# Moving ScalarE's unused elementwise results, the id sums and the row totals from SBUF to PSUM in a segment-mean kernel

## Chip, cores and metric

The kernel runs on one core of one Trainium2 chip. The metric is the device time of one execution in microseconds (us), lower is better. SBUF and PSUM are the two on-chip memories in which tiles are placed (`cpool` and `ppool` below); VectorE, ScalarE and GpSimd are engines, each with its own list of instructions. Most executions of a kernel lie within about 2% here, so kernels were compared on one chip in alternating rounds. A few single runs lay more than 1.5% above the fastest of their kernel; these count as slow, and ranges in brackets show them. Ratios are taken from the fast runs that were not profiled.

## The reference

```python
n, num_segments = 10_000_000, 10000
data = np.random.randn(n).astype(np.float32)
segment_ids = np.sort(np.random.randint(0, num_segments, n))     # int64, sorted

sums, counts = np.zeros(num_segments), np.zeros(num_segments)    # float32
np.add.at(sums, segment_ids, data)
np.add.at(counts, segment_ids, 1)
return sums / np.maximum(counts, 1)
```

The ids are sorted, so each segment is one contiguous stretch of about 1000 values.

## The kernel before

Each of the 128 partitions holds 78,125 consecutive values and works on them as 90 rows of 875 (the last has 250). A row holds at most one border between two segments in the ordinary case, so per row two numbers are enough: the total of the row, and the sum of the part before the border. To find the border, the kernel does not read all ids. It reads five probes per row, a *first look* at them on VectorE gives a position, GpSimd gathers 175 ids there, ScalarE sums these ids, and from the sum a *second look* on VectorE gives the exact border. Then a *split* on VectorE sums the data before the border, while ScalarE makes the row's total.

```python
# cut; the constants are put in one line
P, L, W, NR, HALVES = 128, 875, 175, 90, 66
...
GS = cpool.tile([P, NR], FP32, name="GS")          # id sums, one column a row (SBUF)
T = cpool.tile([P, NR], FP32, name="T")            # row totals               (SBUF)
iota = ppool.tile([P, 1024], FP32, name="iota")    # PSUM already
...
junk_v = cpool.tile([P, L], BF16, name="junk_v")
junk_a = cpool.tile([P, L], BF16, name="junk_a")   # elementwise results that nobody reads (SBUF)

def add_ids(r):                                    # ScalarE, line 315
    nc.scalar.activation(
        out=junk_a[:, 0:W], in_=gt32[:, r % RING, 0 : 2 * W : 2], func=ACT.Copy,
        accum_out=GS[:, r : r + 1],
    )

def second_look(a, b):                             # VectorE, line 322
    def s1():
        nc.vector.scalar_tensor_tensor(
            out=KK[:, a:b], in0=YY[:, a:b], scalar=float(S // K), in1=GS[:, a:b],
            op0=ALU.mult, op1=ALU.subtract,
        )
        ...

def total(r):                                      # ScalarE, line 335
    ...
    d = tiles[r // 2][:, (r % 2) * L : (r % 2) * L + n]
    t = T[:, r : r + 1]
    nc.scalar.activation(out=junk_a[:, 0:n], in_=d, func=ACT.Copy, accum_out=t)

def split(r):                                      # VectorE, line 340
    ...                                            # n and d as in total
    nc.vector.scalar_tensor_tensor(
        out=junk_v[:, 0:n], in0=iota[:, 0:n], scalar=KK[:, r : r + 1], in1=d,
        op0=ALU.is_lt, op1=ALU.mult, accum_out=A[:, r : r + 1],
    )
```

The totals are read by VectorE in few places: once early (line 410), four times in `sums` (`B = T - A`, line 584) and twice at the very end in `inject` (line 751).

```python
# order of the loop (cut): rows of ids run 6 rows ahead of the data (5 rows from row 66 on)
for r in range(..., NR):
    ...                                            # loads of probes and data run further ahead
    while r >= -1 and gs < NR and gs <= r + x_sum(gs):
        add_ids(gs); gs += 1
    if r >= 0:
        total(r)
        split(r)
        for f in after[r]:                         # a second look every 6 rows, every 3 from row 66 on;
            f()                                    # first looks, later stages, the output
```

A second look for rows `a..b-1` stands after the split of row `a-1`. Waits between engines are put in by the framework, from which instruction touches which tile. For PSUM the unit is a bank (here, a tile of 2 KiB per partition): a reader of one column also waits for writes to the others. For an SBUF tile the waits go by columns (e8). Each `activation` with `accum_out` runs as two instructions, an ACTIVATE and an accumulator read (ACTIVATION_READ_ACCUMULATOR) that delivers the sum.

Of the kernel before, what the change touches and what calls it, by code (L numbers as in the profile page):

```python
# [9 lines left out]
FP32 = mybir.dt.float32  # L10
BF16 = mybir.dt.bfloat16
# [6 lines left out]
P = 128  # L18
D = 78125
L = 875  # L20
S = 175
K = L // S
NR = 90
# [95 lines left out]
def kernel(  # L119
# [16 lines left out]
    cpool = ctx.enter_context(tc.tile_pool(name="cpool", bufs=1))  # L136
# [3 lines left out]
    ppool = ctx.enter_context(tc.tile_pool(name="ppool", bufs=1, space=bass.MemoryType.PSUM))  # L140
# [100 lines left out]
    ST = cpool.tile([P, NR], FP32, name="ST")  # L241
    YY = cpool.tile([P, NR], FP32, name="YY")
    IDX = cpool.tile([P, NR], I32, name="IDX")
    GS = cpool.tile([P, NR], FP32, name="GS")
    T = cpool.tile([P, NR], FP32, name="T")
    tl = cpool.tile([P, 1], FP32, name="tl")
    NBP = cpool.tile([P, NX + 1], FP32, name="NBP")
    NB = NBP[:, 1:]
# [3 lines left out]
    nc.vector.memset(NBP, 0.0)  # L252
    nc.vector.memset(FFP[:, 0:1], 0.0)
    junk_v = cpool.tile([P, L], BF16, name="junk_v")
    junk_a = cpool.tile([P, L], BF16, name="junk_a")

    def first_look(g):

# [55 lines left out]
    def add_ids(r):  # L314
# [5 lines that stand above are left out]
    def second_look(a, b):  # L320
# [4 lines that stand above are left out]
# [6 lines left out]
    def total(r):  # L331
        n = min(L, D - r * L)
# [3 lines that stand above are left out]
# [71 lines left out]
    def extend():  # L407

        def s1():
            nc.vector.tensor_sub(out=B[:, 0:E], in0=T[:, 0:E], in1=A[:, 0:E])  # L410
            nc.vector.tensor_copy(out=V[:, 0 : E + 1], in_=VI[:, 0 : E + 1])
            edges(0, E)
# [168 lines left out]
    def sums(a, b, weigh=True, upto=NR):  # L581
        def s1():
            c = min(b, upto)
            nc.vector.tensor_sub(out=B[:, a:c], in0=T[:, a:c], in1=A[:, a:c])  # L584

# [163 lines left out]
    def inject(r, wt, wa, o):  # L749
        return [  # L750
            lambda: v.scalar_tensor_tensor(  # L751
                out=most, in0=wt, scalar=T[:, r : r + 1], in1=most, op0=ALU.mult, op1=ALU.add
            ),
# [158 lines left out]
```

## Time and profile before

| | before |
|---|---|
| median of 3 runs (lowest to highest) | 189.5 us (188.91 to 191.78) |
| profiled run / its span | 188.19 us / 186.4 us |
| VectorE busy / ScalarE busy | 140.8 us / 136.6 us |
| data rate in most slices up to 172 us | 300 to 345 GB/s |
| a ScalarE row (two ACTIVATEs and two reads) | 1.54 us |
| the last second look starts | 173.49 us |

The costliest groups, the waits and part of the tail stand in the prediction. Two more views belong to the reading. The first is the strip of the page: 40 slices of the span, each digit the busy share of a slice in tenths; then, from the list of DMA issues, the gathers with their median time from issue to landing.

```profile
DVE  6321397979197796858879997686899989999881
ACT  8010599967999497895959949599886786989940
...
GT<-in_segment_ids_dram,IDX POOLq DMA_INDIRECT x90, 6.4
```

From slice 7 to slice 27 both engines have slices that are full beside slices that are not, as engines have that wait for each other in a ring (first look, gather, id sums, second look). From slice 29 on VectorE is nearly full. The second view is the timeline around one second look of that tail, the one ahead of row 75; columns are start, length, engine, line, operation, and in brackets the idle time just before with what ended it.

```profile
156.99 0.33 DVE L322 SCALAR_TENSOR_TENSOR q<-YY,GS 128x3 f32<-128x3 f32 x1
...
157.31 0.94 ACT L335 ACTIVATE junk_a<-data_t 128x875 bf16<-128x875 f32 x1
157.36 1.13 DVE L340 SCALAR_TENSOR_TENSOR junk_v<-iota,q,data_t 128x875 bf16<-128x875 f32 x1
...
158.15 0.19 ACT L335 ACTIVATION_READ_ACCUMULATOR junk_a<-data_t 128x1 f32 x1
```

VectorE begins the second look at 156.99 without an idle time. ScalarE's total of row 74, which stands before it in the program, begins only at 157.31 and is complete at 158.34. Nothing ties the two: VectorE is 1.35 us ahead.

### The profile page before, as it was taken

Reading aid. Unit: us, or ns where it says so; the run is one execution under the profiler, and the core shown is the slowest. Engines: PE = TensorE matmul, PEld = TensorE weight load, DVE = VectorE, ACT = ScalarE, POOL = GpSimd, SP = SyncE. Lnnn points to the kernel's source line nnn. Section 1 sums busy time; section 2 is a strip of 40 time slices with the busy share of each in tenths; the row PEclk is TensorE's granted clock in tenths of the full one; section 3 lists DMA queues with packets and bytes.
Section 4 is the critical chain, followed back from the end, with each engine's and each line's share of the span. In section 5 each row is a group of like instructions: output and inputs, shape, how many; then the busy total and the mean of one; then the engine's idle time right before and its main releaser. Section 6 shows DMA issues by size and latency. Waiting matters only on the chain.

```text
span 186.4 us, 1479 instructions
## 1 busy us (share of the span) xinstructions
PE 1.6 (1%) x6; PEld 1.4 (1%) x6; DVE 140.8 (76%) x438; ACT 136.6 (73%) x362; POOL 99.9 (54%) x119
## 2 busy tenths in 40 slices
PE   0000000000002000000000000000000000010000
PEld 0000000000001000000000000000000000010000
DVE  6321397979197796858879997686899989999881
ACT  8010599967999497895959949599886786989940
POOL 5687775076734828266471664727347287883000
DMA  6999999999999999999999999999998999999000
GB/s 28 178 178 340 331 325 328 306 341 330 316 330 319 338 333 305 326 335 332 314 310 335 318 328 317 329 344 307 326 246 246 343 405 406 405 406 391 15 0 12
DMA packets 70613, 54.63 MB, mean 293 GB/s; under 512 B 60464, under 2 KB 61032, under 8 KB 70599
## 3 DMA queue, kind: packets, MB, share of 16 engines
q1 hardware_dynamic: 64667, 40.50, 73.8%
q0 software_dynamic: 5760, 14.01, 23.5%
q14 instruction: 14, 0.11, 0.2%
q10 hardware_dynamic: 172, 0.00, 0.1%
HBM read 56.59 MB, written 0.04 MB: 304 GB/s over the span
## 4 chain that ended last, share of the span: by engine, by line
DMA 33%; issue 32%; ACT 14%; POOL 13%; DVE 4%; POOLq 1%; ACTq 0%
DMA GT<-in_segment_ids_dram,IDX 23%; POOL GT L305 12%; DMA data_t<-in_data_dram 10%; ACT junk_a L335 9%; ACT junk_a L315 5%; POOLq L305 1%; DVE jj L236 0%; POOL i_i L198 0%; DVE junk_v L340 0%; DVE most L745 0%; DVE add L737 0%; POOL pb L703 0%; DVE sel L648 0%; DVE most L751 0%; POOL KL L689 0%
## 5 line engine op out<-in xcount | busy, mean ns | idle before, releaser
L305 POOL DMA_INDIRECT GT<-in_segment_ids_dram,IDX x90 | 90.9, 1010 | 66.9 <-ACT junk_a L315 33.5
L340 DVE SCALAR_TENSOR_TENSOR junk_v<-iota,q,data_t 128x875 bf16<-128x875 f32 x90 | 100.6, 1118 | 8.0 <-DMA data_t<-in_data_dram 6.7
L335 ACT ACTIVATE junk_a<-data_t 128x875 bf16<-128x875 f32 x90 | 83.6, 929 | 3.7 <-DMA data_t<-in_data_dram 0.7
L315 ACT ACTIVATE junk_a<-GT 128x175 bf16<-128x175 int32 x90 | 32.4, 360 | 38.1 <-DMA GT<-in_segment_ids_dram,IDX 35.9
L322 DVE SCALAR_TENSOR_TENSOR q<-YY,GS 128x6 f32<-128x6 f32 (+1 forms) x19 | 3.3, 171 | 21.7 <-ACT junk_a L315 21.7
L315 ACT ACTIVATION_READ_ACCUMULATOR junk_a<-GT 128x1 f32 x90 | 16.8, 187 | 0.0
L335 ACT ACTIVATION_READ_ACCUMULATOR junk_a<-data_t 128x1 f32 x90 | 16.8, 186 | 0.0
L340 DVE DVE_READ_ACCUMULATOR junk_v<-iota,q,data_t 128x1 f32 x90 | 7.4, 83 | 0.0
L272 DVE TENSOR_REDUCE SG<-pr 128x6 f32<-128x30 int32 x15 | 2.7, 180 | 5.7 <-DMA snt<-in_segment_ids_dram 3.3
L281 DVE TENSOR_SCALAR far<-ST 128x6 f32<-128x6 f32 x15 | 2.7, 178 | 0.5
L187 ACT ACTIVATE GT<-q 128x3150 int32<-128x3150 f32 x1 | 3.0, 2996 | 0.0
L284 DVE TENSOR_TENSOR ST<-ST,far 128x6 f32<-128x6 f32 x15 | 2.6, 170 | 0.5
L288 DVE SCALAR_TENSOR_TENSOR IDX<-ST,wb 128x6 int32<-128x6 f32 (+2 forms) x16 | 2.6, 165 | 0.5
L275 DVE SCALAR_TENSOR_TENSOR ST<-pr,SG 128x6 f32<-128x6 int32 x15 | 2.5, 166 | 0.5
L291 DVE SCALAR_TENSOR_TENSOR YY<-ST,SG 128x6 f32<-128x6 f32 x15 | 2.4, 161 | 0.0
L187 ACT ACT_TABLE_LOAD x1 | 1.3, 1283 | 0.7 <-PEq L896 0.7
L584 DVE TENSOR_TENSOR q<-T,q 128x44 f32<-128x44 f32 (+3 forms) x4 | 0.7, 178 | 1.4 <-ACT junk_a L335 1.4
L704 POOL TENSOR_SCALAR pb<-pb 128x168 f32<-128x168 f32 (+1 forms) x2 | 1.6, 784 | 0.2
L544 PE MATMUL badp<-bads,ones 128*128 128x1 f32 x2 | 0.6, 362 | 104.7 <-DVE bads L543 104.7
L236 DVE CAST jj<-jj_i 128x128 f32<-128x128 int32 x1 | 0.8, 840 | 0.7 <-POOL jj_i L235 0.7
L571 DVE RECIPROCAL ct<-ct 128x16 f32<-128x16 f32 (+2 forms) x4 | 1.2, 300 | 0.1
L544 PEld LDWEIGHTS badp<-bads,ones 128*128 128x128 f32 x2 | 0.5, 310 | 104.8 <-DVE bads L543 104.8
(129 smaller groups left out, 45.2 us busy)
## 6 DMA issues: line engine op xcount, KB each, us to landing
data_t<-in_data_dram SPq DMA_DIRECT2D x44, 875.0 KB, 10.6
GT<-in_segment_ids_dram,IDX POOLq DMA_INDIRECT x90, 6.4
pr<-in_segment_ids_dram SPq DMA_DIRECT2D x41, 10.0 KB, 8.1
data_t<-in_data_dram SPq DMA_DIRECT2D x1, 437.5 KB, 18.6
data_t<-in_data_dram SPq DMA_DIRECT2D x1, 125.0 KB, 15.8
out_dram<-OUT SPq DMA_DIRECT2D x1, 36.6 KB
pr<-in_segment_ids_dram SPq DMA_DIRECT2D x1, 31.0 KB, 4.0
snt<-in_segment_ids_dram ACTq DMA_DIRECT2D x1, 1.0 KB
```

The source lines that it names most:

```text
L187: nc.scalar.activation(out=gt32[:, :, 0 : 2 * W : 2], in_=view(q5[:, 0, 0:1], [[0, RING], [0, W]]), func=ACT.Copy)
L272: v.tensor_reduce(out=SG[:, a:b], in_=pr32[:, a:b, 0 : 2 * K : 2], axis=AX.X, op=ALU.add)
L275: v.scalar_tensor_tensor(out=ST[:, a:b], in0=VI[:, a + 1 : b + 1], scalar=float(K), in1=SG[:, a:b], op0=ALU.mult, op1=ALU.subtract,)
L281: v.tensor_scalar(out=far, in0=ST[:, a:b], scalar1=0.0, scalar2=FAR, op0=ALU.is_equal, op1=ALU.mult)
L284: v.tensor_add(out=ST[:, a:b], in0=ST[:, a:b], in1=far)
L288: v.scalar_tensor_tensor(out=IDX[:, c:d], in0=ST[:, c:d], scalar=float(w), in1=wb[:, c:d], op0=ALU.mult, op1=ALU.add)
L291: v.scalar_tensor_tensor(out=YY[:, a:b], in0=ST[:, a:b], scalar=float(K + 1), in1=SG[:, a:b], op0=ALU.mult, op1=ALU.add)
L305: nc.gpsimd.indirect_dma_start(out=GT[:, r % RING, :], out_offset=None, in_=ids2d[:], in_offset=bass.IndirectOffsetOnAxis(ap=IDX[:, r : r ...
L315: nc.scalar.activation(out=junk_a[:, 0:W], in_=gt32[:, r % RING, 0 : 2 * W : 2], func=ACT.Copy, accum_out=GS[:, r : r + 1],)
L322: nc.vector.scalar_tensor_tensor(out=KK[:, a:b], in0=YY[:, a:b], scalar=float(S // K), in1=GS[:, a:b], op0=ALU.mult, op1=ALU.subtract,)
L335: nc.scalar.activation(out=junk_a[:, 0:n], in_=d, func=ACT.Copy, accum_out=t)
L340: nc.vector.scalar_tensor_tensor(out=junk_v[:, 0:n], in0=iota[:, 0:n], scalar=KK[:, r : r + 1], in1=d, op0=ALU.is_lt, op1=ALU.mult, accum_ ...
```

## The change

The intent is to shorten ScalarE's writes: its unused elementwise results, and the sums that it delivers, are written to PSUM in place of SBUF. `junk_a` becomes a tile of 4 KiB per partition; the id sums and the totals share one tile of 2 KiB, that is, one bank in the sense above. The order of instructions on every engine stays as it was.

```diff
-    GS = cpool.tile([P, NR], FP32, name="GS")
-    T = cpool.tile([P, NR], FP32, name="T")
+    GST = ppool.tile([P, 2, 256], FP32, name="GST")
+    GS, T = GST[:, 0, 0:NR], GST[:, 1, 0:NR]
...
-    junk_a = cpool.tile([P, L], BF16, name="junk_a")
+    junk_a = ppool.tile([P, 1024], FP32, name="junk_a")
```

## The prediction

> **What bounds the kernel now.** I read the page first: busy shares, the DMA row, the costliest groups.
>
> ```profile
> PE 1.6 (1%) x6; PEld 1.4 (1%) x6; DVE 140.8 (76%) x438; ACT 136.6 (73%) x362; POOL 99.9 (54%) x119
> ...
> DMA  6999999999999999999999999999998999999000
> ...
> L340 DVE SCALAR_TENSOR_TENSOR junk_v<-iota,q,data_t 128x875 bf16<-128x875 f32 x90 | 100.6, 1118 | 8.0 <-DMA data_t<-in_data_dram 6.7
> L335 ACT ACTIVATE junk_a<-data_t 128x875 bf16<-128x875 f32 x90 | 83.6, 929 | 3.7 <-DMA data_t<-in_data_dram 0.7
> L315 ACT ACTIVATE junk_a<-GT 128x175 bf16<-128x175 int32 x90 | 32.4, 360 | 38.1 <-DMA GT<-in_segment_ids_dram,IDX 35.9
> L322 DVE SCALAR_TENSOR_TENSOR q<-YY,GS 128x6 f32<-128x6 f32 (+1 forms) x19 | 3.3, 171 | 21.7 <-ACT junk_a L315 21.7
> L315 ACT ACTIVATION_READ_ACCUMULATOR junk_a<-GT 128x1 f32 x90 | 16.8, 187 | 0.0
> L335 ACT ACTIVATION_READ_ACCUMULATOR junk_a<-data_t 128x1 f32 x90 | 16.8, 186 | 0.0
> ```
>
> No compute engine is full. The DMA engines are busy in nearly every slice up to 172 us, but busy queues alone do not say what ends a step. VectorE (DVE) idles 21.7 us before the second look (L322, it needs id sums) and only 6.7 us for data; ScalarE (ACT) idles 35.9 us for gathered ids. So I read who waited for whom:
>
> ```profile
> ACT junk_a L315 <- DMA GT<-in_segment_ids_dram,IDX: 35.9, 24, 6.4
> POOL GT L305 <- ACT junk_a L315: 33.5, 21, 5.8
> ...
> DVE q L322 <- ACT junk_a L315: 21.7, 10, 6.9
> DVE junk_v L340 <- DMA data_t<-in_data_dram: 6.7, 12, 0.8
> ```
>
> This is a ring: VectorE computes gather positions (first look), GpSimd issues the gather, it lands (median 6.4 us in the page's DMA part), ScalarE sums the ids, VectorE's L322 uses the sums and can split the next six rows. Up to about 150 us the ring and the DMA rate are nearly level: data arrives 0.3 to 0.8 us before VectorE would otherwise be ready. After 152.3 us VectorE never waits for data again, and the tail is VectorE's own work plus ScalarE. The timeline of the tail matters most:
>
> ```profile
> 173.49 0.16 DVE L322 SCALAR_TENSOR_TENSOR q<-YY,GS 128x3 f32<-128x3 f32 x1
> ...
> 175.46 0.93 ACT L335 ACTIVATE junk_a<-data_t 128x875 bf16<-128x875 f32 x1
> ...
> 176.30 0.19 ACT L335 ACTIVATION_READ_ACCUMULATOR junk_a<-data_t 128x1 f32 x1
> ...
> 177.57 0.17 DVE L584 TENSOR_TENSOR q<-T,q 128x10 f32<-128x10 f32 x1 [0.80 <-ACT junk_a L335]
> ```
>
> Columns are start and length in us. Counting L335 from row 0, the one at 175.46 is the total of row 86; it is complete at 176.49. VectorE did the last second look, which stands after its split of row 86, at 173.49. VectorE runs **3.0 us ahead** of ScalarE here, and nothing stops it.
>
> **What the Trainium skill says.** "ScalarE: Activation LUTs", Step-by-step: "ScE→PSUM is faster than ScE→SBUF". "Perfetto Trace Analysis", Optimizing Scalar/DVE Operations, gives about 93 ns of access for ScalarE on SBUF and 51 on PSUM, and about 60 for DVE on SBUF against 125 on PSUM. The trace has no ScalarE write to PSUM, so the 42 ns are an estimate from that page. The DVE half agrees: L340 reads iota from PSUM and takes 1130 ns for 875 elements, 219 over 875/0.96; the same operation on SBUF alone, L514, takes 273 for 110 elements, 158 over: 61 ns apart. "PSUM — Partial Sum Buffer", PSUM bank collisions raise a hardware error, says two engines must not touch one bank of the same quadrant at once, even at different columns, and to guard by bank. The trace of before cannot show that, but the changed program's waits do.
>
> **The change part by part.**
>
> (a) ScalarE's 180 ACTIVATEs and 180 accumulator reads now write PSUM. In the trace an accumulator read starts 0.10 us before its ACTIVATE ends (0.36 long, read at +0.26), so the ACTIVATE's write tail is hidden already; the read's tail is exposed, because the next ACTIVATE waits for it (0.03 us gap). I count 42 ns per pair: 84 ns off a row of 1.54 us, 180 x 0.042 = 7.6 us of ScalarE work over the run.
>
> (b) VectorE reads id sums and totals from PSUM: 19 L322, L410, 4 L584, 2 L751 = 26 x 0.065 = 1.7 us.
>
> (c) **New waits.** The id sums GS and the totals T are put in one 2 KiB tile, one bank. In the built program's order with its waits, the dependence is by bank. In before, L322 waits for the last id sum of its group; after, each L322 but the first waits for ScalarE's whole total of the row VectorE has just split. And ScalarE, which never waited for VectorE in the loop before, now waits for VectorE's read (L322, L410, L584 or L751) in 25 places before it may write the bank. So every six rows, and every three from row 66 on, both engines meet: a barrier.
>
> Ring, up to 140 us: the path ScalarE to L322 grows by a total and its read, 0.84 + 0.19 = 1.03 us; add 0.065 for the PSUM read; ScalarE's stretch in the ring is six rows, 12 pairs x 0.042 = 0.50 saved. Net about +0.6 us each turn. A turn spans two groups (first look, gather, sums, second look), 22.3 us as L322 recurs in the timeline; five turns lie between 30 and 140 us: **+3.0 us**.
>
> Tail: take the time between second looks at rows 68, 71, 74, 77, 80, 83, 86 for each engine in before. VectorE's L322 starts at 145.67, 151.16, 156.99, 161.33, 165.42, 169.38, 173.49, so its steps are 5.49, 5.83, 4.34, 4.09, 3.96, 4.11. ScalarE's totals end at 146.72, 151.85, 158.34, 162.96, 168.21, 172.83, 176.49: 5.13, 6.49, 4.62, 5.25, 4.62, 3.66. In lockstep each step takes the longer: 5.49+6.49+4.62+5.25+4.62+4.11 = 30.6. Each handover costs L322 with its PSUM read and two semaphore steps, 0.3 us: 1.8 in six. Savings on the ScalarE steps, six pairs each, 0.25 x 4 = 1.0 off. The total of row 68 ended at 146.72, so row 86 meets at 146.72 + 3.0 + 30.6 + 1.8 - 1.0 = 181.1, in place of L322 at 173.49. From L322 to VectorE's end before were 8.79 us, 0.80 of them a wait for ScalarE at L584 which falls away; 0.2 is added for PSUM reads: 181.1 + 8.2 = 189.3 against 182.28. Sum: **+7.0 us**. I take 0.5 off, as late gathers let data run ahead and later gathers may land sooner.
>
> **The rivals.**
>
> Rival 1, ScalarE becomes faster and the kernel with it. For: ScalarE is 73% busy and stands in the ring; without the new waits the ring would turn 0.5 us sooner. Against: data waits of up to 0.8 us at split show DMA close behind, so even then the gain is about 0 to 1 us, 189 us. To win with the waits, a pair would have to save 0.15 us or more.
>
> Rival 2, nothing moves, because DMA is the bound: it is 9 of 10 busy to 172 us and no byte changes. Then about 190 us. Against: the last data lands at 173.4 and VectorE works until 182.3; the lead it loses lies in that tail, which no transfer hides.
>
> Rival 3, the saving is smaller than 42 ns (source still SBUF, fp32 in place of bf16 written). Ring +1.1 a turn, 5.5, tail about +5: about 200 us.
>
> Rival 4, the accumulator read and the ACTIVATE each show their full 42 ns. Ring about +0.1 a turn, tail 1 us less: 193 us.
>
> **Range and chances.** The gain is worked out in the profiled span (186.4) and laid on the unprofiled median: 189.5 + 7.0 - 0.5 = 196.0. The saving per pair is the widest unknown (0 to 0.09 us moves the result from about 200 to 193); add 1 us of run spread (188.91 to 191.78 before). Range 191.8 to 200. Slower by over 2% means over 193.3: chance 0.84; within 2%: 0.14; faster: 0.02.
>
> **What would show it.** Right if: accumulator reads fall from 187 to about 145 ns and ACTIVATEs shorten; L322 waits for L335 in place of L315; ScalarE shows new idle time ended by DVE L322 and L584; VectorE's idle before L322 rises from 21.7 to over 30 us; the last L322 comes near 180 us; the split waits for data almost vanish, as DMA then leads. Wrong if ScalarE pairs shrink by over 0.15 us, so that ScalarE arrives first at each barrier, or if the gathers land much sooner than 6.4 us once loads lead, which would shorten the ring by itself.

## The result and the profile after

The changed kernel took 194.9 us in the median (194.0 to 195.27, 4 runs), against 189.45 (188.91 to 191.78, 4 runs). A ratio in this document is the mean time of one kernel's fast runs over that of the other's in the same rounds, so it is not quite the ratio of the medians. Here it is 1.0272, with a 95% interval of 1.0214 to 1.0331: slower.

First the groups of the page. Columns: line, engine, operation, output and inputs, shapes, count, then busy us and mean ns of one, then idle time ahead with its main releaser.

```profile
PE 1.6 (1%) x6; PEld 1.4 (1%) x6; DVE 140.9 (73%) x438; ACT 126.0 (65%) x362; POOL 99.6 (51%) x119
...
L340 DVE SCALAR_TENSOR_TENSOR junk_v<-iota,q,data_t 128x875 bf16<-128x875 f32 x90 | 100.6, 1118 | 5.6 <-DMA data_t<-in_data_dram 4.2
L335 ACT ACTIVATE junk_a<-data_t 128x875 f32<-128x875 f32 x90 | 80.8, 898 | 9.2 <-DVE most L751 2.5
L315 ACT ACTIVATE junk_a<-GT 128x175 f32<-128x175 int32 x90 | 29.6, 329 | 52.8 <-DMA GT<-in_segment_ids_dram,IDX 44.4
L322 DVE SCALAR_TENSOR_TENSOR q<-YY,GST 128x6 f32<-128x6 f32 (+1 forms) x19 | 3.0, 159 | 30.3 <-ACT junk_a L335 23.5
L315 ACT ACTIVATION_READ_ACCUMULATOR junk_a<-GT 128x1 f32 x90 | 11.5, 128 | 0.0
```

ScalarE's busy time fell by 10.6 us (136.6 to 126.0) and VectorE's stayed, yet the profiled span rose from 186.4 to 193.5 us. All of it is idle time of VectorE: span minus busy time was 45.6 us and is 52.6 us. The profiled run of before was one of the quicker of its kind (188.19), so the span overstates the loss: 2.72% of 189.5 is 5.2 us.

The view of the waits names the new idle time. Columns: engine, tile and line that waited, for what; us in total, times, longest.

```profile
DVE q L322 <- ACT junk_a L335: 23.5, 14, 4.8
...
DVE q L322 <- ACT junk_a L315: 6.8, 1, 6.8
ACT junk_a L315 <- DVE q L322: 4.6, 9, 1.8
DVE junk_v L340 <- DMA data_t<-in_data_dram: 4.2, 4, 1.4
ACT junk_a L335 <- DVE most L751: 2.5, 1, 2.5
ACT junk_a L335 <- DVE q L584: 2.4, 1, 2.4
```

Before, the second look (L322) waited for ScalarE's id sums (L315). Now it waits for the row total (L335), whose result it does not use. In the other direction ScalarE waits for VectorE in 12.4 us of idle time, which did not exist before.

The same second look as shown of before, ahead of row 75, in the timeline:

```profile
162.45 0.90 ACT L335 ACTIVATE junk_a<-data_t 128x875 f32<-128x875 f32 x1
163.29 0.13 ACT L335 ACTIVATION_READ_ACCUMULATOR junk_a<-data_t 128x1 f32 x1
163.45 0.16 DVE L322 SCALAR_TENSOR_TENSOR q<-YY,GST 128x3 f32<-128x3 f32 x1 [2.41 <-ACT junk_a L335]
163.64 0.33 ACT L315 ACTIVATE junk_a<-GT 128x175 f32<-128x175 int32 x1 [0.23 <-DVE q L322]
163.64 1.13 DVE L340 SCALAR_TENSOR_TENSOR junk_v<-iota,q,data_t 128x875 bf16<-128x875 f32 x1
...
181.26 0.15 DVE L322 SCALAR_TENSOR_TENSOR q<-YY,GST 128x3 f32<-128x3 f32 x1
...
184.85 0.90 ACT L335 ACTIVATE junk_a<-data_t 128x875 f32<-128x875 f32 x1 [2.44 <-DVE q L584]
```

VectorE stands for 2.41 us until the total of row 74 is complete at 163.42, then ScalarE stands 0.23 us until VectorE has read the bank. Of the 18 second looks that have a total ahead of them, 14 wait like this, and each of the 14 starts 0.03 us after its total is complete. At the other four VectorE comes later than ScalarE. In before, the nine second looks of rows 6 to 65 that wait at all start 0.03 us after the last id sum of their own group, 1.02 us ahead of that total's end. The last second look starts at 181.26 in place of 173.49.

### The profile page after: what moved, and what is told of

Same layout as the page of the kernel before. It is cut to its first block, busy times and chain, and to the rows that moved or that the text cites. A ratio compares the mean times of both kernels' runs of the same rounds, so it can differ in the third digit from the quotient of the medians.

```text
span 193.5 us, 1479 instructions
## 1 busy us (share of the span) xinstructions
PE 1.6 (1%) x6; PEld 1.4 (1%) x6; DVE 140.9 (73%) x438; ACT 126.0 (65%) x362; POOL 99.6 (51%) x119
## 4 chain that ended last, share of the span: by engine, by line
DMA 32%; issue 29%; ACT 18%; DVE 9%; POOL 8%; SPq 0%; POOLq 0%; ACTq 0%; DVEq 0%
DMA GT<-in_segment_ids_dram,IDX 29%; ACT junk_a L335 11%; POOL GT L305 7%; ACT junk_a L315 7%; DVE junk_v L340 4%; DMA data_t<-in_data_dram 3%; DVE jj L236 1%; DVE q L322 1%; POOL i_i L198 0%; SPq L171 0%; DVE most L745 0%; DVE add L737 0%; POOLq L305 0%; DVE q L584 0%; DVE OUT L745 0%
## 5 line engine op out<-in xcount | busy, mean ns | idle before, releaser
L340 DVE SCALAR_TENSOR_TENSOR junk_v<-iota,q,data_t 128x875 bf16<-128x875 f32 x90 | 100.6, 1118 | 5.6 <-DMA data_t<-in_data_dram 4.2
L335 ACT ACTIVATE junk_a<-data_t 128x875 f32<-128x875 f32 x90 | 80.8, 898 | 9.2 <-DVE most L751 2.5
L315 ACT ACTIVATE junk_a<-GT 128x175 f32<-128x175 int32 x90 | 29.6, 329 | 52.8 <-DMA GT<-in_segment_ids_dram,IDX 44.4
L322 DVE SCALAR_TENSOR_TENSOR q<-YY,GST 128x6 f32<-128x6 f32 (+1 forms) x19 | 3.0, 159 | 30.3 <-ACT junk_a L335 23.5
L315 ACT ACTIVATION_READ_ACCUMULATOR junk_a<-GT 128x1 f32 x90 | 11.5, 128 | 0.0
L335 ACT ACTIVATION_READ_ACCUMULATOR junk_a<-data_t 128x1 f32 x90 | 11.5, 128 | 0.0
L340 DVE DVE_READ_ACCUMULATOR junk_v<-iota,q,data_t 128x1 f32 x90 | 7.5, 83 | 0.0
L737 POOL TENSOR_TENSOR xa<-pa,RG 128x528 f32<-128x528 f32 x1 | 1.2, 1241 | 1.6 <-DVE RG L734 1.6
L236 DVE CAST jj<-jj_i 128x128 f32<-128x128 int32 x1 | 1.5, 1481 | 0.7 <-POOL jj_i L235 0.7
L584 DVE TENSOR_TENSOR q<-GST,q 128x44 f32<-128x44 f32 (+3 forms) x4 | 0.7, 177 | 1.4 <-ACT junk_a L335 1.3
L590 DVE TENSOR_TENSOR_SCAN FFP<-NBP,FFP,XX 128x16 f32<-128x16 f32 (+2 forms) x4 | 1.1, 264 | 0.5 <-DVE q L322 0.5
```

The lines of the kernel that those rows point to most:

```text
L236: nc.vector.tensor_copy(out=jj, in_=jj_i)
L315: nc.scalar.activation(out=junk_a[:, 0:W], in_=gt32[:, r % RING, 0 : 2 * W : 2], func=ACT.Copy, accum_out=GS[:, r : r + 1],)
L322: nc.vector.scalar_tensor_tensor(out=KK[:, a:b], in0=YY[:, a:b], scalar=float(S // K), in1=GS[:, a:b], op0=ALU.mult, op1=ALU.subtract,)
L340: nc.vector.scalar_tensor_tensor(out=junk_v[:, 0:n], in0=iota[:, 0:n], scalar=KK[:, r : r + 1], in1=d, op0=ALU.is_lt, op1=ALU.mult, accum_ ...
```

## The experiments

Ten kernels were run after the changed one; all gave correct results. The theory: the loss is the wait for the newest total, which a shared bank forces on VectorE, part of it in the ring (rows up to 65) and part in the tail. In some traces below, releasers are named "issue" where before a wait for ids had stood, so idle times by cause are compared with care. Totals are named wrongly too: in e1 and e3, where no second look depends on a total, 4.6 and 6.3 us of its idle time are put down to the totals' line. The timeline shows these second looks starting 0.03 us after their own last id sum, a microsecond before the total ends. So a releaser's name is checked against the times.

### Which of the parts costs: the elementwise results alone, the sums alone

e1_junk_only takes over only the `junk_a` line of the diff:

```diff
-    junk_a = cpool.tile([P, L], BF16, name="junk_a")
+    junk_a = ppool.tile([P, 1024], FP32, name="junk_a")
```

> Only the unused elementwise results go to PSUM; id sums and totals stay in SBUF, so the built program has the waits of before. Theory (the shared bank's waits cost the time): ACTIVATE means 903 and 328 ns as in the changed kernel, accumulator reads still 187 ns, row period of ScalarE unchanged at 1.54 us because the ACTIVATE's write tail was already hidden, time 189 us, ratio to before 0.99 to 1.005. Rival (writing fp32 results to PSUM beside VectorE's PSUM reads of iota slows the engines): ratio 1.015 to 1.03.

Measured: 190.1 us (189.29 to 191.89), ratio 1.0005 (0.9949 to 1.0061). From its groups:

```profile
L335 ACT ACTIVATE junk_a<-data_t 128x875 f32<-128x875 f32 x90 | 80.8, 898 | 4.6 <-remote 1.8
L335 ACT ACTIVATION_READ_ACCUMULATOR junk_a<-data_t 128x1 f32 x90 | 16.8, 186 | 0.0
```

The ACTIVATE is as short as in the changed kernel (898 ns, from 929), but ScalarE's busy time is 136.5 us, the 136.6 of before. The record ends 31 ns earlier and the read begins when it did, so nothing is won: what is shortened was hidden under the read already.

e2_sums_only takes over the other part, the shared bank with its waits, and leaves `junk_a` in SBUF:

```diff
-    GS = cpool.tile([P, NR], FP32, name="GS")
-    T = cpool.tile([P, NR], FP32, name="T")
+    GST = ppool.tile([P, 2, 256], FP32, name="GST")
+    GS, T = GST[:, 0, 0:NR], GST[:, 1, 0:NR]
```

> Only the id sums and totals go to PSUM, one bank, with all the waits of the changed kernel; the elementwise results stay bf16 in SBUF. Theory (waits): accumulator reads about 128 ns, ACTIVATE back at 360 and 935 ns, time as the changed kernel, 194 to 196 us, ratio 1.02 to 1.035; last second look near 181 us. Rival (the elementwise PSUM writes cost the time): ratio 0.99 to 1.005.

Measured: 196.99 us (194.15 to 197.15), ratio 1.0279 (1.0189 to 1.037). The waits and the groups:

```profile
DVE q L322 <- ACT junk_a L335: 26.9, 13, 4.5
```
```profile
L315 ACT ACTIVATION_READ_ACCUMULATOR junk_a<-GT 128x1 f32 x90 | 14.1, 157 | 0.0
```

The sums in a shared bank carry the loss; that it is all of it is as sure as the interval, which rests on two runs of e2 (at 2% its verdict is "unclear"). Two expectations were missed: the last second look came at 183.05 and not near 181, and the reads were not 128 ns. The accumulator read took 157 ns here, 128 in the changed kernel and 186 with the elementwise result alone in PSUM: its length depends on where *both* results go.

### Is it PSUM, or the shared bank: banks that are not shared

e3_two_id_banks starts from the changed kernel. The id sums alternate between two banks from one second look to the next, and the totals go back to SBUF. To make room, two small PSUM tiles (`ext`, `badp`) are merged into one bank.

```diff
-    GST = ppool.tile([P, 2, 256], FP32, name="GST")
-    GS, T = GST[:, 0, 0:NR], GST[:, 1, 0:NR]
+    GSA = ppool.tile([P, 512], FP32, name="GSA")
+    GSB = ppool.tile([P, 512], FP32, name="GSB")
+    T = cpool.tile([P, NR], FP32, name="T")
...
+    def gsum(a, b):      # used for GS in add_ids and second_look
+        return (GSB if look_of(a) % 2 else GSA)[:, a:b]
```

> Elementwise results and id sums in PSUM, but the id sums alternate between two banks by second look, and the totals stay in SBUF. VectorE's second look again waits for the last id sum alone, and ScalarE's wait for VectorE lies a group back and should never bind. Theory (waits): ratio 0.985 to 1.0, 186.5 to 189.5 us; accumulator reads 128 ns for ids, 187 for totals; ScalarE idle ended by VectorE under 0.5 us in all. Rival (PSUM sums themselves are slow for VectorE): ratio over 1.01.

Measured: 189.63 us (188.68 to 190.41), ratio 0.9963 (0.9915 to 1.001). ScalarE was busy for 131.2 us, 5.4 less than before, and the kernel is not faster outside the interval. Reads were 128 and 186 ns as expected. "Under 0.5 us" of ScalarE's idle time ended by VectorE does not hold by the names: 2.8 us before one id sum are put down to a split, whose result no id sum uses.

e6_own_banks keeps all three results in PSUM, but gives the id sums and the totals a bank each:

```diff
-    GST = ppool.tile([P, 2, 256], FP32, name="GST")
-    GS, T = GST[:, 0, 0:NR], GST[:, 1, 0:NR]
+    GS = ppool.tile([P, 512], FP32, name="GS")[:, 0:NR]
+    T = ppool.tile([P, 512], FP32, name="T")[:, 0:NR]
```

> All of the change, but id sums and totals each in a bank of their own (the two small matmul results share one bank to make room). ScalarE still waits for VectorE's reads in 25 places; VectorE's second look waits for the last id sum alone. Theory (it is VectorE's wait for the total that costs, since VectorE is ahead): ratio 0.99 to 1.004, VectorE 2 us or more ahead at the last second look. Rival (ScalarE's new waits for VectorE cost as much): ratio 1.012 or more.

Measured: 190.56 us (189.76 to 191.49), ratio 1.0078 (1.0023 to 1.0132): 1.9 points of the 2.7 are gone, but the middle lies above the range that the theory gave. The waits show the second look back on the id sums:

```profile
DVE q L322 <- ACT junk_a L315: 22.4, 9, 7.0
```

The expected lead of VectorE at the last second look, 2 us or more, was missed: it was 0.3 us (177.09 against 177.43). What was left was first put down, as an argument, to the totals' own bank (ScalarE's last totals still wait 2.3 and 2.5 us for L584 and L751). The trace shows another wait, which the expectation above denies. From row 66 on the id sums run ahead of their group, and the second look waits for the newest one in the bank. Ahead of row 69, for example, it needs the sums of rows 69 to 71, complete at 142.90; it starts when that of row 73 is complete (counting L315 from row 0):

```profile
147.23 0.13 ACT L315 ACTIVATION_READ_ACCUMULATOR junk_a<-GT 128x1 f32 x1
...
147.39 0.16 DVE L322 SCALAR_TENSOR_TENSOR q<-YY,GS 128x3 f32<-128x3 f32 x1 [0.52 <-ACT junk_a L315]
```

Five second looks of the tail start so, 0.03 us after an id sum that is two rows newer than any they use, and VectorE idles 2.3 us before them (1.2 us of it, ahead of row 75, is named L335 in the waits). So one bank for all id sums is still shared, between groups of rows. One more run was made, e9_three_banks: the two alternating banks of e3 for the id sums, and a bank of its own for the totals. To make room, it also moves a matmul result into the merged bank, in a branch that this data does not take.

```diff
-    T = cpool.tile([P, NR], FP32, name="T")            # of e3_two_id_banks
+    T = ppool.tile([P, 512], FP32, name="T")
```

> The same PSUM residence as the change for all three results, but in banks that are not shared: id sums alternate between two banks by second look, the totals have a third. Theory (the loss is the wait for the newest total, made by the shared bank): L322 idles by about 21 us for id sums alone, ratio to before 0.993 to 1.003. Rival A (a totals bank of its own still costs, as the run with one bank each for id sums and totals showed 1.0078): ratio 1.005 to 1.01, with L584 and L751 as the places. Rival B (shorter ScalarE pairs must show once the waits are gone): ratio under 0.98.

Measured, in 5 rounds: 189.96 us (188.64 to 190.82), ratio 1.0001 (0.9945 to 1.0057). That is the theory's range, and rival B is out: ScalarE is busy for 126.0 us, 10.6 less than before, and the time is the same. Rival A is not borne out either, since the totals have their own bank here too, and ScalarE's last total waits 2.5 us for L751 as it did. Whether e6 and e9 really differ in time stays open: the intervals overlap. The wait of e6 is gone: in e9 four of the same five second looks start before that newer id sum is complete, and VectorE has no idle time before any second look of the tail. The expected 21 us of idle time before the second look was missed:

```profile
DVE junk_v L352 <- DMA data_t<-in_data_dram: 13.2, 20, 1.2
DVE q L334 <- ACT junk_a L327: 13.2, 6, 6.7
```

(L352 is the split and L334 the second look in this kernel.) VectorE's wait for id sums fell from 21.7 to 13.2 us, and its wait for data rose from 6.7 to 13.2: 28.4 us together before, 26.4 here. This fits data being next in line, but it is one profile: in e3, in the same time and with 5.4 us less of ScalarE, the two waits are 29.3 and 1.0 us. What a faster ScalarE runs into is not shown; that it wins no more than 0.6% here is.

### Where it costs: ring or tail

e4_tail_free uses the shared bank only for the id sums of rows under 66 and the totals of rows under 62, and SBUF after; e5_tail_only is the reverse. In both, `junk_a` is in PSUM.

```diff
+    GSP, TP = GST[:, 0, 0:NR], GST[:, 1, 0:NR]
+    GSS = cpool.tile([P, NR], FP32, name="GSS")
+    TS = cpool.tile([P, NR], FP32, name="TS")
...
+    def gsum(a, b):
+        return (GSP if a < 66 else GSS)[:, a:b]     # e5: (GSS if a < 66 else GSP)
...
+    def tt(a, b):
+        return (TP if a < 62 else TS)[:, a:b]       # e5: (TS if a < 62 else TP)
```

> The changed kernel up to row 65 (sums and totals in the shared bank, with the waits); later rows' sums and totals (totals from row 62) in SBUF without new waits. Theory: keeps only the ring's share, about +2 to +3 us of the +5.4: 191.5 to 192.5 us, ratio 1.008 to 1.018, VectorE ahead of ScalarE again by 2 us or more at the last second look. Rival (all of the loss is made in the tail): ratio 0.995 to 1.004. Rival (all is made in the ring before 140 us): ratio 1.025 or more.

> The mirror of the tail-free run: sums and totals in SBUF up to row 65 (totals 61), then in the shared bank with its waits. Theory (ring and tail add up): the remaining share, +2.5 to +4 us, 192.5 to 194 us, ratio 1.012 to 1.022; VectorE's lead over ScalarE at the last second look gone, ScalarE's last two totals held back 2.4 us each. Rival (the ring's delay is what makes the tail late): ratio under 1.006.

Measured: e4 192.06 us (191.39 to 193.59), ratio 1.0113 (1.0046 to 1.0179); e5 192.59 us (190.43 to 193.82), ratio 1.0121 (1.0033 to 1.0209), from only two runs that are fast and not profiled (190.43, 192.16; at 2% its verdict is "unclear"). The second look (L333 in these) by its two halves, first of e4, then of e5:

```profile
L333 DVE SCALAR_TENSOR_TENSOR q<-YY,GST 128x6 f32<-128x6 f32 x11 | 1.8, 161 | 29.5 <-ACT junk_a L346 22.2 <-issue 7.3
L333 DVE SCALAR_TENSOR_TENSOR q<-YY,GSS 128x3 f32<-128x3 f32 x8 | 1.4, 178 | 0.0
```
```profile
L333 DVE SCALAR_TENSOR_TENSOR q<-YY,GSS 128x6 f32<-128x6 f32 x11 | 1.8, 165 | 20.9 <-ACT junk_a L326 10.3 <-issue 6.8 <-ACT junk_a L346 3.8
L333 DVE SCALAR_TENSOR_TENSOR q<-YY,GST 128x3 f32<-128x3 f32 x8 | 1.2, 155 | 3.1 <-ACT junk_a L346 3.1
```

In e4 VectorE has no idle time at all before its second looks of the tail, and at the last one (177.23) it is again 3.1 us ahead of the total of row 86 (180.29), as before. In e5 it is 0.5 us behind (179.01 against 178.54). Both halves cost about the same, 2.1 and 2.3 us of 189.5, and 1.13% with 1.21% make up the 2.72% within the intervals. These are wide: that of e5 reaches down to 1.0033 and does not shut out its rival (under 1.006), against which only the lost lead of VectorE speaks.

### The wait without PSUM

e7_wait_in_sbuf has nothing in PSUM that before had not. A tiny copy ahead of each second look but the first reads the total of the row just split. ScalarE waits for nobody.

```diff
+    seen = cpool.tile([P, 1], FP32, name="seen")
...
+            if a:
+                nc.vector.tensor_copy(out=seen, in_=T[:, a - 1 : a - 0])
             nc.vector.scalar_tensor_tensor(
```

e8_copy_control is the same with a total six rows older, `T[:, a - 6 : a - 5]`, long complete when it is read: the copy without its wait.

> The kernel before, all in SBUF, with one small VectorE copy of the newest total ahead of each second look but the first: VectorE must wait for the same totals as in the changed kernel, without any PSUM write and without ScalarE waiting for VectorE. Theory: slower by as much or more, since no accumulator read is shortened: ratio 1.025 to 1.045, 194.5 to 198 us. Rival (the loss needs PSUM): ratio as the control, 1.0 to 1.01.

> Control: the same 18 copies of a total that is six rows old, so that nothing waits. All theories: ratio 1.0 to 1.01 (18 copies of about 0.15 us, 2.7 us of VectorE work, most of it in idle time up to 140 us, eight copies or about 1.2 us in the tail).

Measured: e7 198.22 us (198.08 to 199.5), ratio 1.0509 (1.0437 to 1.058); e8 189.13 us (188.69 to 189.92), ratio 0.9999 (0.9934 to 1.0063). The copy, first of e7, then of e8:

```profile
L324 DVE COPY seen<-T 128x1 f32<-128x1 f32 x18 | 2.7, 153 | 31.6 <-ACT junk_a L338 28.5 <-issue 3.0
```
```profile
L324 DVE COPY seen<-T 128x1 f32<-128x1 f32 x18 | 2.7, 148 | 0.0
```

The copies cost nothing, the wait alone costs more than the whole change: a one-sided wait of VectorE for the newest total is a sufficient cause. It is larger than expected. The copy itself explains some of that: in e7's tail the split starts 0.29 us after the end of the total, in the changed kernel 0.22, so 18 copies add 1.3 us to the path. The rest, some 3 us of the 4.5 between the two kernels, fits ScalarE's rows being 0.12 us longer than in the changed kernel (21 rows from 66 on are 2.5 us). That is an argument and not shown; e2, whose reads are also longer, was not slower than the changed kernel, though its interval (1.0189 to 1.037) is too wide to decide it.

### Keep the bank, move one instruction

If the loss is how *new* the total is that VectorE waits for, then the order can mend it. e10_total_after_look is the changed kernel, and in each row that a second look follows, that row's total is issued after it:

```diff
         if r >= 0:
-            total(r)
-            split(r)
+            meet = (r + 1) % 6 == 0 or (r >= HALVES and (r + 1) % 3 == 0)
+            if meet and r < NR - 1:
+                split(r)
+                after[r].pop(0)()        # the second look
+                total(r)
+            else:
+                total(r)
+                split(r)
```

> The changed kernel with its shared bank, but in a row that a second look follows the row's split and the second look are issued ahead of that row's total. So the second look needs the total of the row before only, and ScalarE's total of this row waits for the second look. Theory (the loss is how new the total is that VectorE must wait for): L322's idle before it falls from 30 us to 20 to 25, ratio to before 1.005 to 1.02. Rival (any handshake of both engines at a second look costs the same, or ScalarE held back costs more than VectorE held back): ratio 1.025 or more.

Measured, in 5 rounds: 191.29 us (190.82 to 193.12), ratio 1.0083 (1.0026 to 1.0139), where 1.005 to 1.02 was expected. The waits:

```profile
DVE q L322 <- ACT junk_a L315: 14.4, 11, 6.4
DVE junk_v L340 <- DMA data_t<-in_data_dram: 13.2, 15, 1.7
```
```profile
ACT junk_a L335 <- DVE q L322: 9.5, 18, 2.4
```

The bank is still shared and the engines still wait for each other, now ScalarE for VectorE in 18 places. VectorE no longer waits for a total at the second look, and 1.9 of the 2.7 points are back. L322's idle time fell below the 20 to 25 us that was expected, to 14.4, while the wait for data rose to 13.2. The rival, that a handshake costs the same whichever engine is held, is out. What is left, 0.8%, goes with the wait of e6: in the tail VectorE idles 1.6 us for an id sum two rows newer than it needs, which the shared bank still imposes. How much of the 0.8% that makes was not tested.

No version here is faster than the kernel before: the best, e3, has an interval that reaches 1.001.

## Why the prediction was right

The side and the mechanism held, and the time was 194.9 against 196.0. By its steps:

- **The new wait** is as described. L322 waits for L335, ScalarE has idle time ended by L322 and L584, and the idle time ahead of L322 rose from 21.7 to 30.3 us. That last sign is weaker than the prediction made it: e1 shows 29.9 us of it, with part put down to "issue", at ratio 1.0005, since waits for data and for ids trade places. The sum of both tells more: 28.4 us before, 30.3 in e1, 34.5 after. Of the 25 places where the prediction has ScalarE wait for VectorE, 17 show idle time, 12.4 us in all. One reading in the prediction is the wrong way round: up to 150 us data does not arrive 0.3 to 0.8 us before VectorE is ready, it is VectorE that waits for it (12 times, 0.8 us at most). The working does not rest on it.
- **Step (a), the saving of ScalarE**, was mis-sized. It counted 42 ns a pair, an estimate from "Perfetto Trace Analysis", Optimizing Scalar/DVE Operations, in the Trainium skill. Measured are 59 ns off the read (187 to 128) and none off the path from the ACTIVATE, whose tail was hidden, as the step said. A row went from 1.54 to 1.42 us, which is 60 ns a pair.
- **Step (b), VectorE's reads from PSUM**, was wrong. It added 65 ns to each of 26. L322 took 159 ns after and 171 before, L584 177 and 178, L751 about 247 and 245. (One long record of 0.33 us lifts the 171; without it the mean is about 162.) So the 1.7 us do not exist, and the comparison that was to confirm the 61 ns does not carry over to these reads. The 0.96 elements per ns in it fit L340's own two lengths (1130 ns for 875 elements, 474 for 250: 1.05 ns an element), but L340 also differs from L514 in its output type and in summing its result, so the 61 ns need not be PSUM's.
- **Step (c), ring and tail**, was right in kind and too large: +3.0 and +4.0 us were predicted, e4 and e5 show 2.1 and 2.3. With the measured sizes put in, the same working gives less: a ring path longer by 0.84 + 0.13 and shorter by 12 x 0.06 makes +0.25 a turn, 1.3 us in five. In the tail six handovers of 0.22 cost 1.3, and four times six pairs of 0.06 save 1.4, so the last meeting is at 146.72 + 1.3 + 30.6 + 1.3 - 1.4 = 178.5, and 8.0 us later the end, +4.2 us. The measured 5.2 us have an interval of 4.1 to 6.3 (2.14% to 3.31% of 189.5): the corrected +4.2 lies in it, the +6.5 just above it. So the saving per pair, the handover and the PSUM reads, all mis-sized, are enough to explain the excess. The lockstep itself held step by step: in the profile after, ScalarE ends steps two to five of the tail and VectorE the first and the sixth, as forecast, and the six take 30.6 us, where 31.4 were worked out.
- **The last second look** came at 181.26, predicted 181.1. This is luck in part. In the profile after, the first L322 was already 0.87 us late, before any second look waits for a total, and profiles of kernels of equal time (e1, e3) have L322 at row 60 later than before by 3.0 and 2.9 us and still end within 1.7 us of it. One profile's position in the ring is good to some 3 us; the ratios of e4 and e5 are what carries the split into ring and tail.
- **Waits for data** were to almost vanish; they fell from 6.7 to 4.2 us. Gathers did not land sooner (6.5 us after, 6.4 before), so the 0.5 us taken off for that had no ground.
- **Rival 1** (a faster ScalarE) and **rival 2** (DMA hides it) were rightly set aside for this kernel, but without the shared bank the outcome is theirs: in e9 ScalarE's 10.6 us are saved and the time is the same (1.0001). Rivals 3 and 4 fall with step (a): the saving was larger than 42 ns and smaller than 84.

## What to carry to other kernels

Before moving results of one engine into PSUM, look at which bank each reader's data shares with what is still being written: two results in one bank make a reader wait for the newest write of either, and the slower engine's lag becomes the other's. Give them banks of their own, or issue the write that nobody needs yet after the read. A bank of its own is not enough for a result whose later columns are written before the earlier ones are read (e6): let it alternate between two banks (e3, e9). And read the lead of one engine over another in the timeline: where nothing ties them that lead is worth time, and a saving on an engine that is not the bound does not pay for its loss.

## What the Trainium skill lacked or had wrong

- "Perfetto Trace Analysis", Optimizing Scalar/DVE Operations, gives one access cost for ScalarE on each memory. Here the cost of a sum depends on both results: the accumulator read took 187 ns with both in SBUF, 186 with only the elementwise result in PSUM, 157 with only the sum there, 128 with both. No page looked up here says how long an accumulator read takes.
- The same section puts a VectorE access at about 125 ns on PSUM and 60 on SBUF. For small operations with one operand moved to PSUM no rise was seen: 159 against 171 ns (L322), 177 against 178 (L584).
- "ScalarE: Activation LUTs", Step-by-step, says that "ScE→PSUM is faster than ScE→SBUF". For the elementwise result of an ACTIVATE that is followed by an accumulator read, the record is shorter (898 against 929 ns) and the time is the same (ratio 1.0005), which the page does not say.
- "PSUM — Partial Sum Buffer", PSUM bank collisions raise a hardware error, says to guard by bank, and has no word on what the guard costs when two results that do not depend on each other share one: ratio 1.0272 here, against 1.0001 in three separate banks and 1.0083 with the write issued after the read.
